# Decode attention and recurrent heads on TensorE: which small products stand next to each other

## The chip, the cores and the metric

The kernel runs on one core of a Trainium2 chip. The metric is the device time of one execution in microseconds (us), from the launch to the end on the core. TensorE (PE) multiplies matrices, VectorE (DVE) and ScalarE (ACT) work on tiles in SBUF and PSUM, GpSimd (POOL) issues the gathers, SyncE (SP) most other DMAs. Each engine has its own stream of instructions and takes them in the order in which the program holds them; semaphores tie the streams together.

## The reference, cut to what matters

One layer of a hybrid decoder, for 512 prompt tokens and for 8 sequences with 4 new tokens each (32 sample tokens), in fp32: a half feed-forward block, a mixer, another half feed-forward block.

```python
h = h + 0.5 * rmsnorm(swiglu(rmsnorm(h, g0), wg[0], wu[0], wd[0]), g1)
m = mixer(rmsnorm(h, g2), ...)          # 4 recurrent heads and 4 latent-attention heads
h = h + rmsnorm(m, g3)
h = h + 0.5 * rmsnorm(swiglu(rmsnorm(h, g4), wg[1], wu[1], wd[1]), g5)
```

Two parts of the mixer matter here. A recurrent head (key and value dimension 128) works in chunks of 64 tokens; within a chunk

```python
b = cumsum(logf)                                   # logf, q, k: (tokens, 128)
A[t, s] = sum_k exp(b[t] - b[s]) * q[t] * k[s]     # s <= t
o = A @ v + (q * exp(b)) @ S                       # S: the state before the chunk
S = exp(b_last) * S + (k * exp(b_last - b)).T @ v
```

The sample tokens of the latent attention see 4096 earlier tokens, held in pages and found through a page table:

```python
keys_c = cache_kv_latent[page_table]     # (8, 4096, 256)
keys_r = cache_k_rope[page_table]        # (8, 4096, 64)
s = (q_lat @ keys_c.T + q_rope @ keys_r.T) / sqrt(192)
o_lat = softmax(s) @ keys_c              # 16 rows (4 tokens, 4 heads) for each sequence
```

## The kernel before, in words

Large products keep fp32 precision by splitting each operand into a high and a low part and adding three products (`mm3`, `gemm_q`, L248). So each weight tile is loaded by SP (`wraw`), rounded by ACT (`wh`) and subtracted by DVE (`wl`, L222); these products, called GEMMs or column products here, are nearly all of TensorE's work. The order of the work is the order in which Python generators are advanced: small work (heads, decode) is placed between pieces of a large one by hand. Some PSUM banks rotate: the list `CYC` gives four banks in turn for all small products (`ps`).

**The recurrent heads** (`hgrn`, L876 on). A head has three generators. `pre` makes q, k, b, v and the gate from column products (512 prompt tokens and 32 sample tokens in two parts of 272), with the transposes of v (L912). `levels` makes A. Since exp(b[t]-b[s]) cannot be split into factors without overflow over a whole chunk, the chunk is split again and again: for each of the decay levels m = 32, 16, 8, 4, 2, 1, `scaled(m)` (L939 to L951) makes a tile `g_E` whose first half of each pair of blocks of m tokens holds k scaled and whose second half holds q scaled; eight products of 64x32 tiles (L971) then give the part of A in which t lies in a second block and s in the first one. Level 0 is the diagonal (L973). Predicated copies put the parts into A (L983, L985), and with products of 32x32 (L977) and copies (L987) the same is done for the sample tokens. The levels are taken in three runs, `RUNL`, each followed by a `yield`; the tiles of the next run are made ahead of the products of the present one, and `g_E` has EB = 4 buffers. `tail` turns k (L1010), makes the states (`pS`, L1026), A times v (L1035), the rest of o, and for the sample tokens the eight state updates (L1069). The function `four` (L888) puts a transpose of the 32 sample tokens on each of the four groups of 32 partitions: once for v in `pre`, once for k in `tail`. The loop over heads advances `levels` and `tail` of one head by one step and then the next head's `pre` by PAT[step] pieces, so that TensorE has column products between the small runs.

**The decode** (L1450 on). The 8 x 4096 past keys are 32 blocks of 1024; a `Half` n (16 of them) is two blocks, half of one sequence. Its life is spread over several rounds of the loop `decode` (L1567 on), each round having five steps st = 0 to 4. In round n:

- `gather` (L1469, POOL, an indirect DMA of 1 MB) fetches a block of latent rows into one of seven slots, `gather_r` (L1476) the rotary keys. After the first ones a block is fetched behind the values that free its slot.
- `turn` (L1484) turns ten groups of 32 key dimensions, two a step in the order `JS`, into `kh`: two DVE transposes of 128x512 (one for each block) a step. The rotary groups come first (`rraw`). `kh` has KHB = 4 buffers, so a turn waits for the scores of four steps earlier.
- `score` (L1496) multiplies the turned keys with the queries, 64x32 tiles, 16 products a step, for half n-2. The table `RUNS` says in which step of the round which of the five scores are issued: three (48 products) at step 2, two (32 products) at step 4. Behind the last, the sums are copied out (L1502, one on ACT, one on DVE) and DVE takes the maximum of each partition (L1504).
- `peak` at step PEAK = 1, for half n-3: TensorE turns the maximum to all partitions (`pm`, L1508, 128x128), DVE reduces it (L1510) and scales it (L1513), ACT takes the exponent (L1514), DVE turns the result (`pt`, L1516), and sixteen copies fill `pbuf` (L1520, four on DVE and twelve on ACT). 
- `value` at step 4, for half n-3: `o`, 2 x 8 products with the latent rows (L1529), and behind the products of each block the next `gather`. For every second half two small products (L1537) and a copy (L1538) follow beside the next `peak`.

A steady round is thus on TensorE: o, some GEMMs, pm, some GEMMs, 48 score products, some GEMMs, 32 score products, the next o. The GEMMs come from `phase_a` (out-projection, first columns of the second feed-forward block, 512 wide), which the main loop (L1627 on) advances beside the decode by a quota for each step (PRE, BODY). `turn` is called at the end of each step; at step 4 it is tied to stand behind the maximum on DVE (`issue_after`). The pipeline starts one turn a step from round 1, step 1, with a gap at round 2: the condition `if n != 2 or st >= 2` leaves out its steps 0 and 1.

## Time and profile before

| | |
|---|---|
| median of three runs | 1236.41 us (1235.94 to 1236.56) |
| the profiled execution | 1235.82 us |
| its span, first to last instruction | 1234.0 us, so 1.8 us lie around it |
| mean granted TensorE clock | 0.995 |
| PE busy over the span | 1207.3 us, 98% |
| DVE busy over the span | 980.4 us, 79% |
| ACT busy over the span | 702.6 us, 57% |
| moved by all DMA in the span | 190.70 MB |

How to read it: the page's parts are the span, each engine's busy time, the span in forty slices, the DMA queues, the shares of the chain that ended last, and the costliest groups of instructions. The timeline lists instructions with their start in us from the span's start, their duration, engine, line, operation, output tile and inputs, tile size, shape and count. A product of two fp32 operands leaves two records for one instruction, so counts of small products are doubled there. Matmuls are pipelined and the end of each is modelled, so the distance from start to start says more than the duration.

### The profile page before, as it was taken

How to read it: one execution, taken by the hardware profiler on the slowest of the kernel's cores; microseconds unless marked ns; L12 is line 12 of the kernel's file. 1: busy time of each engine (PE TensorE's matmuls, PEld its weight loads, DVE VectorE, ACT ScalarE, POOL GpSimd, SP SyncE). 2: the span in 40 equal slices, each digit the busy share in tenths (PEclk: the TensorE clock that was granted, in tenths of full speed). 3: DMA queues.
4: the chain of work that ended last, by engine and by line, in shares of the span. 5: the costliest groups of instructions: out<-in, count | busy, mean ns of one | idle time of the engine just before them, and what ended most of it. 6: DMA issues, size and time to landing. Idle time of an engine off the chain costs nothing.

```text
span 1234.0 us, 29432 instructions
## 1 busy us (share of the span) xinstructions
PE 1207.3 (98%) x12216; PEld 1112.1 (90%) x12216; DVE 980.4 (79%) x1994; ACT 702.6 (57%) x1524; POOL 94.8 (8%) x106
## 2 busy tenths in 40 slices
PE   8999999999999999999999899999999999999997
PEld 7999999999999989988898887777777899999996
DVE  7897787878678787885878789998885779778765
ACT  7675545454376654454758766465555456555373
POOL 0000000000000000000000112332320111000000
PEclk9999999999999999999999999999999999999999
DMA  6232332323254313323342586689774776933551
GB/s 240 86 110 96 103 103 91 99 85 104 65 203 134 116 55 104 89 85 110 99 139 77 158 336 206 220 284 354 276 269 155 263 267 226 223 110 108 113 147 74
DMA packets 80519, 190.70 MB, mean 155 GB/s; under 512 B 14065, under 2 KB 37649, under 8 KB 75905
## 3 DMA queue, kind: packets, MB, share of 16 engines
q1 hardware_dynamic: 58128, 115.50, 28.4%
q0 software_dynamic: 16368, 65.67, 16.3%
q10 hardware_dynamic: 5888, 7.65, 1.9%
q8 instruction: 96, 1.57, 0.5%
q14 instruction: 39, 0.31, 0.1%
HBM read 172.63 MB, written 16.16 MB: 153 GB/s over the span
## 4 chain that ended last, share of the span: by engine, by line
PE 81%; DVE 7%; issue 5%; ACT 4%; DMA 3%; POOL 0%; DVEq 0%; SPq 0%; POOLq 0%
PE acc L248 18%; PE dn L230 12%; PE acc L230 10%; PE Y L449 10%; PE X L449 7%; PE Z L449 6%; PE acc L1833 3%; PE acc L627 3%; PE s L1496 3%; PE o L1529 2%; DVE kh L1484 1%; DMA ma<-w_g 1%; PE pa L971 1%; PE s L1224 1%; DMA wraw<-w_u 1%
## 5 line engine op out<-in xcount | busy, mean ns | idle before, releaser
L248 PE MATMUL acc<-uh,wh 128*128 128x272 f32 (+2 forms) x496 | 161.7, 326 | 0.5 <-ACT uh L195 0.5
L248 PE MATMUL acc<-ul,wh 128*128 128x272 f32 (+2 forms) x496 | 156.6, 316 | 0.9 <-DVE ul L196 0.9
L248 PE MATMUL acc<-uh,wl 128*128 128x272 f32 (+2 forms) x496 | 155.6, 314 | 0.0
L230 PE MATMUL dn<-hh,dh 128*128 128x272 f32 x384 | 111.6, 291 | 0.1
L221 ACT CAST wh<-wraw 128x1024 fp32r<-128x1024 f32 (+2 forms) x78 | 72.6, 932 | 67.1 <-PE acc L248 59.6
L230 PE MATMUL dn<-hh,dl 128*128 128x272 f32 x384 | 110.6, 288 | 0.0
L230 PE MATMUL dn<-hl,dh 128*128 128x272 f32 x384 | 110.5, 288 | 0.0
L222 DVE TENSOR_TENSOR wl<-wraw,wh 128x1024 fp32r<-128x1024 f32 (+2 forms) x78 | 83.7, 1074 | 33.7 <-ACT wh L221 32.9
L248 PEld LDWEIGHTS acc<-uh,wh 128*128 128x128 f32 x496 | 93.3, 188 | 15.2 <-issue 10.1
L248 PEld LDWEIGHTS acc<-ul,wh 128*128 128x128 f32 x496 | 93.4, 188 | 7.1 <-issue 1.6
L248 PEld LDWEIGHTS acc<-uh,wl 128*128 128x128 f32 x496 | 93.3, 188 | 6.1 <-issue 1.1
L230 PEld LDWEIGHTS dn<-hh,dh 128*128 128x128 f32 x384 | 72.3, 188 | 1.3 <-DVE hb L498 0.3
L230 PEld LDWEIGHTS dn<-hl,dh 128*128 128x128 f32 x384 | 72.5, 189 | 0.0
L230 PEld LDWEIGHTS dn<-hh,dl 128*128 128x128 f32 x384 | 72.1, 188 | 0.0
L158 ACT CAST wh<-wraw 128x512 fp32r<-128x512 f32 (+1 forms) x67 | 41.0, 650 | 40.0 <-PE Z L449 22.4
L158 ACT CAST sh<-wraw 128x512 fp32r<-128x512 f32 (+1 forms) x66 | 40.6, 657 | 37.6 <-PE Z L449 26.0
L158 ACT CAST dh<-wraw 128x512 fp32r<-128x512 f32 x48 | 29.8, 621 | 45.8 <-PE dn L230 44.2
L159 DVE TENSOR_TENSOR wl<-wraw,wh 128x512 fp32r<-128x512 f32 (+1 forms) x67 | 46.9, 723 | 7.6 <-ACT wh L158 7.1
L1520 ACT COPY pbuf<-pt 32x64 f32<-32x64 f32 x192 | 46.5, 242 | 8.4 <-DVE pt L1516 5.6
L1496 PE MATMUL s<-kh,q 64*32 64x128 f32 x2560 | 49.1, 273 | 2.0 <-issue 2.0
L1496 PEld LDWEIGHTS s<-kh,q 64*32 64x32 f32 x2560 | 37.5, 105 | 13.4 <-issue 8.0
L159 DVE TENSOR_TENSOR sl<-wraw,sh 128x512 fp32r<-128x512 f32 (+1 forms) x66 | 46.6, 733 | 1.9 <-ACT sh L158 0.8
(721 smaller groups left out, 4109.2 us busy)
## 6 DMA issues: line engine op xcount, KB each, us to landing
wraw<-w_u SPq DMA_DIRECT2D x44, 512.0 KB, 4.2
wraw<-w_g SPq DMA_DIRECT2D x43, 512.0 KB, 3.5
wraw<-w_d SPq DMA_DIRECT2D x24, 512.0 KB, 4.4
wraw<-w_in SPq DMA_DIRECT2D x24, 512.0 KB, 3.9
wraw<-w_o SPq DMA_DIRECT2D x16, 512.0 KB, 3.6
wraw<-w_d SPq DMA_DIRECT2D x16, 384.0 KB, 3.1
wraw<-w_d SPq DMA_DIRECT2D x16, 256.0 KB, 4.5
mA<-sit ACTq DMA_DIRECT2D x14, 256.0 KB, 3.1
```

The costliest lines, as they stand in the source:

```text
L158: nc.scalar.copy(hi, src)
L159: (eng or nc.vector).tensor_tensor(lo, src, f32(hi), op=ALU.subtract)
L221: nc.scalar.copy(wh[:, :kt], w[:, :kt])
L222: low[0] = nc.vector.tensor_tensor(wl[:, :kt], w[:, :kt], f32(wh[:, :kt]), op=ALU.subtract)
L230: nc.tensor.matmul(out, a, b, start=n == 0, stop=n == last)
L248: nc.tensor.matmul(acc[:, :n], a[:, k], b[:, k], start=k + i == 0, stop=k == kt - 1 and i == 2)
L449: nc.tensor.matmul(bank, a[p][:, k], b[q][:, k], start=first and k + n == 0, stop=k == 3 and n == 2, skip_group_check=True)
L627: nc.tensor.matmul(accs[x, d], wts[d][p][:, k], hs[k // 2][q][:, k % 2, x], start=k + n == 0, stop=k == nf - 1 and n == 2)
L1496: nc.tensor.matmul(self.s[r][c * 32 : c * 32 + 32, :P], q[rs, j], kh, start=st + jj == 0, stop=st == len(JS) - 1 and jj == 1, skip_group_c ...
L1520: (nc.scalar.copy if g else nc.vector.tensor_copy)(self.p[g * 32 : g * 32 + 32, c // 2, c % 2 * 4 : c % 2 * 4 + 4, self.i * 16 : self.i * ...
L1529: nc.tensor.matmul(o[g : g + 32, :R], self.p[:, c, a], self.craw[c][:, a], start=i + c == 0 and a < 4, stop=i + c == 2 and a >= 4, skip_gr ...
L1833: nc.tensor.matmul(accs[x, d], wts[d][p][:, k], hs[k // 2][q][:, k % 2, x], start=k + n == 0, stop=k == nf - 1 and n == 2)
```

## The change

Two independent edits.

1. The decode: `RUNS` puts the first three scores of half n-2 at step 1, where `peak` of half n-3 stands, and the gap in the turns at round 2 is one step shorter. The last two scores stay at step 4.

2. The recurrent heads: all seven levels are multiplied in one run instead of three. `scaled` is called for all six levels first, with EB = 6 buffers, in three portions with the same number of `yield`s. The gather of the sample tokens' v moves from `pre` to the end of that run, the one of k from the transposes of k to the run of A times v; `gather32` does what `four` and the copy behind it did.

```diff
-EB, RUNL = 4, ((32, 16), (8, 4), (2, 1, 0))
+EB, RUNL = 6, ((32, 16), (8, 4), (2, 1, 0))
-RUNS = {2: (0, 1, 2), 4: (3, 4)}
+RUNS = {1: (0, 1, 2), 4: (3, 4)}
...
-            def four(out, t):
+            def gather32(t, tag):
+                out = ps("tp")
                 for g in range(0, P, TS):
                     nc.tensor.matmul(out[g : g + TS, :P], t[:, TP:], ident, start=True, stop=True, skip_group_check=True)
+                s_ = mk([P, P], F32, tag)
+                nc.scalar.copy(s_, out[:, :P])
+                return s_
...
-                tp = ps("tp")
-                four(tp, v)
-                vs = mk([P, P], F32, "g_vs", 2)
-                nc.scalar.copy(vs, tp[:, :P])
...
-                ops = [scaled(m) for m in RUNL[0]]
-                for i, ms in enumerate(RUNL):
-                    cur = ops
-                    if i + 1 < len(RUNL):
-                        ops = [scaled(m) if m else (k, q) for m in RUNL[i + 1]]
-                    pa = ps("pa")
+                ops = []
+                for ms in RUNL[:-1]:
+                    ops.append([(m, *scaled(m)) for m in ms])
+                    yield
+                ops.append([(m, *(scaled(m) if m else (k, q))) for m in RUNL[-1]])
+                pas = [ps("pa") for _ in range(2)]
...
+                for ms in ops:
+                    for m, kx, qx in ms:
...
+                vs = gather32(H["v"], "g_vs")
+                for m, po in outs:
...
-                tp = ps("tp")
-                four(tp, k)
-                ks = mk([P, P], F32, "g_ks")
-                nc.scalar.copy(ks, tp[:, :P])
...
                     nc.tensor.matmul(o[es, c * P : (c + 1) * P], A[es, c], vn[es, c], start=c == 0, stop=c == 0, skip_group_check=True)
+                ks = gather32(k, "g_ks")
...
-                        if n != 2 or st >= 2:
+                        if n != 2 or st >= 1:
                             turn(at(2).top if at(2) and st == len(JS) - 1 else None)
```

The lines of the decode move up by two (L1484 is L1482 after, L1496 is L1494, L1508 is L1506, L1510 is L1508, L1516 is L1514, L1529 is L1527); of the heads, L971 is L972, L973 is L974, and L888 is L889.

What the edits do to the order is shown at three places. First TensorE in the second recurrent head, at its last run of level products (`pa` is the PSUM tile of A, `acc` that of a column product). Before:

```order
L248 MATMUL acc<-uh,wl 128x272
L971 MATMUL pa<-g_E 64x32 x16
L973 MATMUL pa<-g_q,g_k 64x64 x8
L977 MATMUL pa<-g_E 32x32 x2
L977 MATMUL pa<-g_q,g_k 32x32
L248 MATMUL acc<-uh,wh 128x272
```

And now, at the only run of level products of that head:

```order
L248 MATMUL acc<-uh,wl 128x272
L972 MATMUL pa<-g_E 64x32 x48
L974 MATMUL pa<-g_q,g_k 64x64 x8
L977 MATMUL pa<-g_E 32x32 x2
L977 MATMUL pa<-g_q,g_k 32x32
L889 MATMUL tp<-ident,g_f 32x128 x4
L248 MATMUL acc<-uh,wh 128x272
```

The 32 products of two earlier runs and the gather of v have moved into this one. In the first head eight of the 48 stand apart.

Next TensorE in the decode, around the product that turns the maximum of half 10 (`s` holds the scores, `q_8207` the queries, `acc` a GEMM). Before:

```order
L248 MATMUL acc<-uh,wl 128x512
L1508 MATMUL pm<-ident,mxh 128x128
L1537 MATMUL o<-q_8207,q_8242 128x32 x2
L248 MATMUL acc<-uh,wh 128x512
L248 MATMUL acc<-ul,wh 128x512
L248 MATMUL acc<-uh,wl 128x512
L248 MATMUL acc<-uh,wh 128x512
L248 MATMUL acc<-ul,wh 128x512
L248 MATMUL acc<-uh,wl 128x512
L1496 MATMUL s<-kh,q_8207 32x128 x48
```

And now:

```order
L248 MATMUL acc<-uh,wl 128x512
L1494 MATMUL s<-kh,q_8203 32x128 x48
L1506 MATMUL pm<-ident,mxh 128x128
L1535 MATMUL o<-q_8203,q_8238 128x32 x2
L248 MATMUL acc<-uh,wh 128x512
```

The run of 48 scores has moved past six GEMMs and past pm; it stands directly ahead of pm.

Last DVE in the decode, from the maximum of half 10 to the reduction of its pm and what follows (`kh` are turned keys, `dx0`, `dx1`, `q0`, `ha` slots of gathered blocks, `rraw` rotary keys). Before:

```order
L1504 TENSOR_REDUCE mxh_11399<-q1_8207 128x1
L1484 STREAM_TRANSPOSE kh_11422<-dx0_11009 128x512
L1484 STREAM_TRANSPOSE kh_11422<-dx1_11214 128x512
L1484 STREAM_TRANSPOSE kh_11431<-dx0_11009 128x512
L1484 STREAM_TRANSPOSE kh_11431<-dx1_11214 128x512
L1484 STREAM_TRANSPOSE kh_11468<-dx0_11009 128x512
L1484 STREAM_TRANSPOSE kh_11468<-dx1_11214 128x512
L1510 TENSOR_REDUCE q1_8207<-pm_11440 128x16
L1538 COPY q0_8242<-o_11205 128x4x16
L1513 SCALAR_TENSOR_TENSOR mq_11443,mbd_11444<-q1_8207 128x16
L1516 STREAM_TRANSPOSE pt_11447<-q1_8207 128x256
```

And now:

```order
L1502 TENSOR_REDUCE mxh_11398<-q1_8203 128x1
L1482 STREAM_TRANSPOSE kh_11421<-dx0_11008 128x512
L1482 STREAM_TRANSPOSE kh_11421<-dx1_11213 128x512
L1482 STREAM_TRANSPOSE kh_11430<-dx0_11008 128x512
L1482 STREAM_TRANSPOSE kh_11430<-dx1_11213 128x512
L1482 STREAM_TRANSPOSE kh_11521<-dx0_11008 128x512
L1482 STREAM_TRANSPOSE kh_11521<-dx1_11213 128x512
L1482 STREAM_TRANSPOSE kh_11530<-rraw_11333 128x512
L1482 STREAM_TRANSPOSE kh_11530<-rraw_11335 128x512
L1482 STREAM_TRANSPOSE kh_11554<-q0_8238 128x512
L1508 TENSOR_REDUCE q1_8203<-pm_11493 128x16
L1536 COPY q0_8238<-o_11204 128x4x16
```

Nine transposes instead of six stand between the maximum and the reduction; the tenth, of the second block in `ha`, stands between the reduction and `pt`. Before, the last four of these stood behind `pt` and behind the next maximum.

More of the change, by code (lines that the diff above doesn't have):

```diff
@@ L954, in up @@
                     return t.rearrange("p (n t m) -> p n t m", t=2, m=m)[:, :, 1]
[L956 to L964 removed]
+                ops = []
[4 more added lines that the diff above has]
+                pas = [ps("pa") for _ in range(2)]
+                outs = []
+                col = 0
+                for ms in ops:
+                    for m, kx, qx in ms:
                         w = 32 if m else CH
[L966 removed]
+                        po = pas[col // 512][:, col % 512 : col % 512 + 4 * w].rearrange("p (c t) -> p c t", c=4)
                         col += 4 * w
[L968 removed]
+                        outs.append((m, po))
                         for c, e, es, cs in chunks():
@@ L973, in levels @@
                                 nc.tensor.matmul(po[es, c], kx[:, cs], qx[:, cs], start=True, stop=True, skip_group_check=True)
-                    if min(ms) <= 2:
-                        pb = ps("pa")
-                        for j, (kx, qx) in enumerate(cur):
-                            nc.tensor.matmul(pb[:TS, j * TS : (j + 1) * TS], kx[:, TP:], qx[:, TP:], start=True, stop=True, skip_group_check=True)
-                    for j, (m, po) in enumerate(zip(ms, outs)):
-                        l = (LEVELS + (0,)).index(m)
-                        if m:
-                            Av = A.rearrange("p c (n t m) -> p c n t m", t=2, m=m)[:, :, :, 1]
-                            mv = up(msk[:, l], m)[:, None].broadcast_to([P, 4, CH // (2 * m), m])
-                            nc.vector.copy_predicated(Av, mv, po.rearrange("p c (n m) -> p c n m", m=m))
-                        else:
-                            nc.vector.copy_predicated(A, msk[:, l : l + 1, :].broadcast_to([P, 4, CH]), po)
-                        if m <= 2:
-                            nc.vector.copy_predicated(As, msk[:TS, l, :TS], pb[:TS, j * TS : (j + 1) * TS])
-                    yield
-                H.update(A=A, As=As)
+                pb = ps("pa")
+                for j, (m, kx, qx) in enumerate(ops[-1]):
+                    nc.tensor.matmul(pb[:TS, j * TS : (j + 1) * TS], kx[:, TP:], qx[:, TP:], start=True, stop=True, skip_group_check=True)
+                vs = gather32(H["v"], "g_vs")
+                for m, po in outs:
+                    l = (LEVELS + (0,)).index(m)
+                    if m:
+                        Av = A.rearrange("p c (n t m) -> p c n t m", t=2, m=m)[:, :, :, 1]
+                        mv = up(msk[:, l], m)[:, None].broadcast_to([P, 4, CH // (2 * m), m])
+                        nc.vector.copy_predicated(Av, mv, po.rearrange("p c (n m) -> p c n m", m=m))
+                    else:
+                        nc.vector.copy_predicated(A, msk[:, l : l + 1, :].broadcast_to([P, 4, CH]), po)
+                    if m <= 2:
+                        j = RUNL[-1].index(m)
+                        nc.vector.copy_predicated(As, msk[:TS, l, :TS], pb[:TS, j * TS : (j + 1) * TS])
+                yield
+                H.update(A=A, As=As, vs=vs)
             def rows(o, out, n, m):
```

7 lines of the change are left out of this document (1 added, 6 removed).

## The prediction

> **What bounds the kernel now.** I read the page first: the span, the busy shares, the shares of the chain that ended last.
>
> ```profile
> span 1234.0 us, 29432 instructions
> PE 1207.3 (98%) x12216; PEld 1112.1 (90%) x12216; DVE 980.4 (79%) x1994; ACT 702.6 (57%) x1524; POOL 94.8 (8%) x106
> PE 81%; DVE 7%; issue 5%; ACT 4%; DMA 3%; POOL 0%; DVEq 0%; SPq 0%; POOLq 0%
> ```
>
> TensorE is busy 98% of the span and 81% of the last chain. Time goes only if matmuls go, if the joints between kinds of matmul get cheaper, or if TensorE waits less. The view of windows shows the two stages that are edited, first one period of the recurrent heads, then halves 2 to 13 of the decode. Its columns are the window and its length, the busy time of PE, its weight loads, DVE, ACT and POOL, the granted clock, and the DMA's share and GB/s.
>
> ```profile
> 468.95:506.92 37.97, 37.79 (x418) 34.04 (x417) 30.80 (x74) 18.94 (x42) 0.43 (x2) 1.00 0.27 85
> 762.19:918.06 155.87, 152.77 (x2905) 111.87 (x2904) 138.59 (x318) 86.85 (x259) 49.05 (x50) 1.00 0.78 275
> ```
>
> In the first, PE is short of its window by 0.18 us: nothing is late, DVE has 7 us to spare. In the second PE is short by 3.1 us of 156, and DVE works 138.59, 89%. So the recurrent stage is a sum of PE times; the decode is one too, but with a vector engine nearly as full, whose order decides whether PE waits. The clock is full in both.
>
> **Part 1, the recurrent heads.** Here the timeline of TensorE gives the price of a joint: a run of two level products (16 records) and one of four (32 records) between column products, and the plain cadence.
>
> ```profile
> 427.32 0.29 PE L248 MATMUL acc<-uh,wl 128*128 128x272 f32 x1
> ...
> 430.35 0.29 PE L248 MATMUL acc<-uh,wl 128*128 128x272 f32 x1
> 430.57 0.66 PE L971 MATMUL pa<-g_E 128*64 128x32 f32 x16
> ...
> 431.39 0.29 PE L248 MATMUL acc<-ul,wh 128*128 128x272 f32 x1
> ...
> 473.73 0.29 PE L248 MATMUL acc<-uh,wl 128*128 128x272 f32 x1
> 473.95 1.12 PE L971 MATMUL pa<-g_E 128*64 128x32 f32 x32
> ...
> 475.23 0.29 PE L248 MATMUL acc<-ul,wh 128*128 128x272 f32 x1
> ```
>
> From 427.32 to 430.35 stand 24 column products: 0.126 us each. I price a run from the start of the last column product before it to the start of the second one behind it (the first behind still shows the joint), less two cadences. 16 records: 431.39 - 430.35 - 0.252 = 0.79. 32 records: 475.23 - 473.73 - 0.252 = 1.25. So 16 records more cost 0.46, 0.029 each, and 0.79 - 0.46 = 0.33 is the fixed price of a run. By the order the stage had 44 runs between column products and has 36 now (levels joined, gathers of the 32 sample tokens moved in, less a few that the pS products open, since they now fall on both sides of a column product). 8 x 0.33 = 2.6 us.
>
> The eight gathers of the sample tokens (two a head) also stood in another shape than their neighbours:
>
> ```profile
> 423.31 0.29 PE L248 MATMUL acc<-uh,wl 128*128 128x272 f32 x1
> 423.44 0.38 PE L912 MATMUL tp<-ident,g_f 128*128 128x128 f32 x2
> ...
> 423.78 0.29 PE L248 MATMUL acc<-ul,wh 128*128 128x272 f32 x1
> ...
> 424.42 0.29 PE L248 MATMUL acc<-uh,wh 128*128 128x272 f32 x1
> ...
> 424.86 0.43 PE L888 MATMUL tp<-ident,g_f 128*32 128x128 f32 x8
> ...
> 425.44 0.29 PE L248 MATMUL acc<-uh,wl 128*128 128x272 f32 x1
> ```
>
> Two transposes alone: 423.78 - 423.31 - 0.252 = 0.22. Two transposes and the gather: 425.44 - 424.42 - 0.252 = 0.77. The gather costs 0.55 behind 128x128 products. Inside a run of other small tiles its eight records cost 0.23 by the slope above, at most their own 0.43. So it saves between 0.1 and 0.3; I take 0.2, near the slope, since its new neighbours are such records: 8 x 0.2 = 1.6. Together -4.2 us, from -2.5 (fixed part alone) to -5.
>
> What could take this back: six E tiles must now be made before the first level product, and the ten masked copies come in one burst behind the last. The 7 us that DVE has free per head cover both; without that cover the wait could be a microsecond a head, 4 in all. The k gather goes one step later and its copy is read only by the last products of the head. I cost both at nothing.
>
> **Part 2, the decode: fewer joints.** Before, the product that turns the maximum (pm, 128x128) stands alone and the first run of scores (s, 48 products as 96 records) six GEMMs behind it; now they adjoin. By the order the scores stand ahead of pm, not behind. The trace of before has both forms, the second in half 11, where no GEMM fell between.
>
> ```profile
> 833.46 0.39 PE L248 MATMUL acc<-hh,wl 128*128 128x512 f32 x1
> 833.68 0.38 PE L1508 MATMUL pm<-ident,mxh 128*128 128x128 f32 x2
> ...
> 834.14 0.39 PE L248 MATMUL acc<-hl,wh 128*128 128x512 f32 x1
> ...
> 835.06 0.40 PE L248 MATMUL acc<-hh,wl 128*128 128x512 f32 x1
> 835.39 1.59 PE L1496 MATMUL s<-kh,q 64*32 64x128 f32 x96
> ...
> 837.26 0.39 PE L248 MATMUL acc<-hl,wh 128*128 128x512 f32 x1
> ...
> 882.72 0.40 PE L248 MATMUL acc<-uh,wl 128*128 128x512 f32 x1
> 882.95 0.38 PE L1508 MATMUL pm<-ident,mxh 128*128 128x128 f32 x2
> 883.27 1.59 PE L1496 MATMUL s<-kh,q 64*32 64x128 f32 x96
> ...
> 885.13 0.40 PE L248 MATMUL acc<-ul,wh 128*128 128x512 f32 x1
> ```
>
> Cadence here: 835.06 - 834.14 over four products, 0.23. pm alone: 834.14 - 833.46 - 0.46 = 0.22. Scores alone: 837.26 - 835.06 - 0.46 = 1.74. Together 1.96; adjoining, 885.13 - 882.72 - 0.46 = 1.95. Nothing is saved. In every second half pm has two further small products behind it, so I allow up to 0.1 a half: 0 to -1.5, taken as -0.5, near the row.
>
> The page "TensorEngine Tiling (Array Packing)" of the Trainium skill says, under Tiling Modes, Key Properties, that changing the tiling mode drains TensorE. By it each half should save one change of mode; the rows above show the fixed price of a run, as the rule would have it, but no saving where these two adjoin.
>
> **Part 3, the decode: the chain.** pm feeds a chain whose end the next values need: DVE reduces pm, ACT takes the exponent, DVE turns it (pt), 16 copies fill pbuf, then TensorE runs o. Half 10 on TensorE, DVE and ACT, then half 13:
>
> ```profile
> 870.47 0.38 PE L1508 MATMUL pm<-ident,mxh 128*128 128x128 f32 x2
> 878.20 1.07 PE L1529 MATMUL o<-mb,pbuf 128*32 128x256 f32 x16
> 867.97 3.67 DVE L1484 STREAM_TRANSPOSE kh<-dx 128x512 f32<-128x512 f32 x6
> 871.56 0.25 DVE L1510 TENSOR_REDUCE q<-pm 128x16 f32<-128x128 f32 x1
> 872.76 0.45 DVE L1516 STREAM_TRANSPOSE pt<-q 128x256 f32<-128x256 f32 x1 [0.73 <-ACT q L1514]
> 873.70 3.07 ACT L1520 COPY pbuf<-pt 32x64 f32<-32x64 f32 x12
> 911.49 3.07 ACT L1520 COPY pbuf<-pt 32x64 f32<-32x64 f32 x12 [0.51 <-DVE pt L1516]
> 913.29 1.07 PE L1529 MATMUL o<-hb,pbuf 128*32 128x256 f32 x16
> 914.17 0.86 PE L1529 MATMUL o<-mb,pbuf 128*32 128x256 f32 x12
> ```
>
> The last copies fill rows 4 to 7 of the second block, read from the middle of the second run of o: two runs stand 0.88 apart (913.29, 914.17), so the last copy may end 1.32 after o starts. Half 10: 878.20 + 1.32 - 876.77 = 2.75 us to spare. Half 13: 913.29 + 1.32 - 914.56 = 0.05. It is the tightest half, and has twelve GEMMs between pm and o where half 10 has eighteen.
>
> Now the scores stand ahead of pm, so pm starts 1.74 later against o, and the spare falls by 1.74 less what the chain no longer waits for. That is nothing: on DVE, eight or nine transposes, not six, stand between the maximum and the reduce (scores free their kh buffers sooner). One takes 3.67 / 6 = 0.61, so nine end 5.5 after 867.97, at 873.5; pm, 1.74 later at 872.2, would be reduced at 873.3 if the lag stayed at 871.56 - 870.47 = 1.09. The reduce loses about 0.2, and what follows it 0 to 0.5, as one or two transposes stand between it and pt, mostly under the 0.73 that DVE waits there for ACT. Where a weight split stands there too it is a further microsecond. Queued behind: the reduce for the chain, and behind the chain o, the end of TensorE's half.
>
> Half 10 keeps 2.75 - 1.74 - (0.2 to 0.7) = 0.3 to 0.8: covered, barely. Half 13 lacks 1.7 to 2.4. By the order of after, four of the fourteen steady halves have only twelve GEMMs from pm to the second scores. Half 13 was the tightest, so I estimate 1.25 for each: 5 us. The other ten are like half 10 with a spare near zero, some short where a split stands in the way; 0.25 each, 2.5 us.
>
> Two more effects, both unseen in before. The turn of a half's second block stands up to eight transposes earlier on DVE, ahead of pt. Its gather is issued only behind the half's o:
>
> ```profile
> DMA to landing us min/median/max: 5.4/8.2/13.6
> 868.46 0.95 POOL L1469 DMA_INDIRECT ha<-pool_c,idx  x1 [0.30 <-issue]
> 881.04 0.67 DVE L1484 STREAM_TRANSPOSE kh<-ha 128x512 f32<-128x512 f32 x1
> ```
>
> From issue to use were 12.6 us; at some 5 less, 7.6, a landing at the median of 8.2 is 0.6 late, one of 13.6 by 6. But only landings above 7.6 hurt, and there the reduce ahead may be late anyway: I take 0.5 in all, and keep 0 to 12 for the range. Below nothing: were PE's 3.1 us in this window all waits that the sooner transposes remove, the decode would gain them; I keep -1.
>
> Sum of the decode's chain: 5 + 2.5 + 0.5 = +8, from -1 to +16. The profiled execution took 1235.8 us (span 1234.0 and 1.8 around it), 0.6 below the median of the runs, 1236.4. -4.2 - 0.5 + 8 = +3.3: 1239.1 against the execution, 1239.7 against the median. A difference of 0.2%, 2.5 us, is about what a measurement of this kernel can tell from none: 1233.9 and 1238.9 are the bounds.
>
> **The rivals.**
> Covered chain (0.22): DVE's freed time behind pt (no transposes stand between pbuf and the next maximum any more) lets each half start its chain sooner, and only the joints count: -4.7, 1231.7. For it: PE hardly waits in before; against it: half 13's 0.05.
> A change of mode has its full price (0.05): the 0.33 of part 1 saved in 15 halves, 4.9 in place of 0.5: 1239.7 - 4.4 = 1235.3. Against it stands half 11. It is the rule of the Trainium skill's page on tiling taken at its word.
> Balance (0.19): only the four short halves pay, 5 - 4.7 = +0.3: 1236.7.
> Gathers decide (0.17): where the second block lands after some 7.6 us from its issue, DVE stands at that transpose with pt queued behind. About half of fourteen landings are later, by 0.6 to 6; at 1 us each this adds 7: 1246.7. For it: DMA is busy 0.78 in this window.
> That the change doesn't do what it says applies to part 2: adjoining, it saves nothing; this is in the forecast.
>
> **How the numbers follow.** Forecast, 0.37: 1239.7, from 1237 to 1243, so 0.10 of it within 0.2% and 0.27 above. Covered chain: 0.22 faster. Mode price: 0.02 faster, 0.03 same. Balance: 0.02 faster, 0.14 same, 0.03 slower. Gathers: 0.17 slower. Faster 0.26, same 0.27, slower 0.47. The range leaves out the far halves of the two outer cases: 1230.5 to 1249.
>
> **What would show it.** In the profile after: the four heads shorter by about 1 us each, with PE still busy throughout; adjoining scores and pm at 1.9 to 2.0 together; between the maximum and the reduce 5 to 6 us of DVE; TensorE standing before o for pbuf, in the short halves by 1 us or more; the decode longer by 6 to 9. I am wrong if o never waits (then the covered chain), if DVE's wait ahead of pt names a gather in many halves (then 1247), or if the heads are not shorter, because the E tiles come late.

## The result, and the profile after

Six runs of each kernel: the changed kernel takes 1254.65 us (1252.19 to 1258.15), the kernel before 1236.22 us (1234.69 to 1236.68); the ratio is 1.015, 95% interval 1.0137 to 1.0162. Slower by 18.4 us, where 3.3 were forecast and 1249 was the range's end. The profiled execution took 1252.19 us, the least of the six, and its span is 1250.2; it lies 16.4 us over the profiled execution of before. The page:

```profile
span 1250.2 us, 29449 instructions
PE 1212.9 (97%) x12216; PEld 1107.2 (89%) x12216; DVE 980.2 (78%) x1994; ACT 704.4 (56%) x1524; POOL 92.5 (7%) x106
PE 75%; DVE 8%; issue 7%; ACT 6%; DMA 3%; POOL 0%; DVEq 0%; SPq 0%; ACTq 0%; POOLq 0%
```

The same instructions are done (12216 records of TensorE, 1994 of DVE), TensorE's share of the last chain falls from 81% to 75%. The windows say where. First one head's period in the kernel after, from one run of levels to the next (37.97 us before):

```profile
476.07:513.19 37.12, 37.12 (x417) 33.91 (x416) 30.78 (x75) 19.35 (x42) 0.43 (x2) 1.00 0.29 88
```

Then the decode from the start of o of half 1 to that of half 13, in the kernel before and in the kernel after:

```profile
769.48:913.28 143.80, 140.70 (x2685) 103.13 (x2680) 128.08 (x293) 79.38 (x237) 46.57 (x47) 1.00 0.80 281
```

```profile
767.28:929.00 161.72, 148.54 (x2680) 100.49 (x2680) 129.26 (x298) 81.73 (x243) 43.99 (x46) 1.00 0.73 249
```

A head is 0.85 us shorter and TensorE never waits in it. Twelve halves of the decode are 17.9 us longer with the same work: 13.5 us a half, not 12.0. TensorE stands idle for 13.2 us of them, not 3.1, and DVE is busy 80%, not 89%: no engine is full any more, so the half is bound by a chain of waits. The idle time is 10.1 us of the 17.9. The rest stands in TensorE's busy time though its work is the same, mostly where o takes `pbuf` piece by piece and its records lie farther apart (o is busy 28.5 us in this window, 23.2 before). Priced as in the prediction, which takes both in, the 14 steady runs of 32 scores and o sum to 63.2 us (47.2 before); the 14 of 48 scores, pm and what adjoins to 33.2 (30.4 before; two of them wait a microsecond or more). That is nearly all of the 18.9 us by which the way from o of half 1 to o of half 14 is longer, and 18.9 less the 2.5 that the heads gain is the 16.4.

Half 10 on DVE shows the chain. The first row is its maximum, the last its turned exponent pt:

```profile
879.60 0.42 DVE L1502 TENSOR_REDUCE mxh<-q 128x1 f32<-128x256 f32 x1 [1.97 <-ACT q L1500]
879.94 2.48 DVE L1482 STREAM_TRANSPOSE kh<-dx 128x512 f32<-128x512 f32 x4
882.68 1.30 DVE L1482 STREAM_TRANSPOSE kh<-dx 128x512 f32<-128x512 f32 x2 [0.26 <-PE s L1494]
883.91 1.26 DVE L1482 STREAM_TRANSPOSE kh<-rraw 128x512 f32<-128x512 f32 x2
885.09 0.67 DVE L1482 STREAM_TRANSPOSE kh<-q 128x512 f32<-128x512 f32 x1
885.69 0.25 DVE L1508 TENSOR_REDUCE q<-pm 128x16 f32<-128x128 f32 x1
...
887.09 0.71 DVE L1482 STREAM_TRANSPOSE kh<-ha 128x512 f32<-128x512 f32 x1 [0.93 <-DMA ha<-pool_c,idx]
...
888.29 0.43 DVE L1514 STREAM_TRANSPOSE pt<-q 128x256 f32<-128x256 f32 x1
```

And the same half on TensorE, then ScalarE:

```profile
881.90 1.59 PE L1494 MATMUL s<-kh,q 64*32 64x128 f32 x96
883.43 0.49 PE L1506 MATMUL pm<-ident,mxh 128*128 128x128 f32 x2
...
888.48 1.16 PE L1494 MATMUL s<-kh,q 64*32 64x128 f32 x64
890.18 1.09 PE L1527 MATMUL o<-mb,pbuf 128*32 128x256 f32 x16 [0.55 <-DVE pbuf L1518]
```

```profile
889.05 3.07 ACT L1518 COPY pbuf<-pt 32x64 f32<-32x64 f32 x12
892.14 0.27 ACT L1500 COPY q<-s 128x128 f32<-128x128 f32 x1
```

Four transposes follow the maximum at once, the fifth waits 0.26 us for the score run: there are four `kh` buffers, and the scores that free the next ones now stand directly ahead of pm. From 882.68 on five transposes lie in the way, 3.0 us, and the reduction starts at 885.69, 2.26 us behind pm (1.09 before). The maximum is late as well: it waited 1.97 us for ScalarE's copy of the scores, so pm starts 3.40 us behind its end, where 1.74 more than before would be 4.15. One more transpose, which waits for its gather, stands ahead of pt. pbuf is full at 892.12. Without a wait o would start at 889.6, 1.08 behind the scores as in half 10 of before, and its last copy would be wanted 1.32 later: pbuf is 1.2 us late, and the run of scores and o costs 4.47 us in place of 3.15. And the copy of the scores for the next maximum stands behind the twelve copies of pbuf on ScalarE, at 892.14.

Over halves 1 to 13, start of pm to start of the reduction on the timelines is 2.88 us on average (1.36 before), pm to the last copy of pbuf 8.23 (6.70 before). The later reduction can be taken apart. From the end of the maximum to the reduction DVE's queue takes 6.48 us on average (3.90 before): transposes 4.83 (3.45), other work such as weight splits and the feed-forward block's elementwise products 1.33 (0.53), idle 0.39 (none before; the rows overlap by 0.1). pm starts 3.60 us behind the maximum (2.54 before). So the queue grew by 2.6 us and pm moved back by 1.1. DVE's list of waits in the decode (sum in us, times, longest) has the late maximum far above the transposes that wait for a buffer:

```profile
DVE mxh L1502 <- ACT q L1500: 14.2, 9, 2.4
DVE kh L1482 <- PE s L1494: 1.6, 3, 0.7
```

### The profile page after: what moved, and what is told of

Read it like the earlier page. It is cut to its first block, busy times and chain, and to the rows that moved or that the text cites. A ratio compares the mean times of both kernels' runs of the same rounds, so it can differ in the third digit from the quotient of the medians.

```text
span 1250.2 us, 29449 instructions
## 1 busy us (share of the span) xinstructions
PE 1212.9 (97%) x12216; PEld 1107.2 (89%) x12216; DVE 980.2 (78%) x1994; ACT 704.4 (56%) x1524; POOL 92.5 (7%) x106
## 3 DMA queue, kind: packets, MB, share of 16 engines
q0 software_dynamic: 16368, 65.67, 16.4%
## 4 chain that ended last, share of the span: by engine, by line
PE 75%; DVE 8%; issue 7%; ACT 6%; DMA 3%; POOL 0%; DVEq 0%; SPq 0%; ACTq 0%; POOLq 0%
PE acc L248 15%; PE dn L230 11%; PE Y L449 10%; PE acc L230 9%; PE X L449 7%; PE Z L449 7%; DVE kh L1482 3%; PE acc L1831 3%; PE acc L627 3%; ACT pbuf L1518 3%; DMA ma<-w_g 1%; PE pa L972 1%; PE s L1222 1%; PE s L1494 1%; DMA ha<-pool_c,idx 1%
## 5 line engine op out<-in xcount | busy, mean ns | idle before, releaser
L1494 PEld LDWEIGHTS s<-kh,q 64*32 64x32 f32 x2560 | 38.1, 105 | 17.1 <-issue 8.7
L1494 PE MATMUL s<-kh,q 64*32 64x128 f32 x2560 | 51.4, 273 | 1.6 <-issue 0.6
```

The source lines that it names most:

```text
L1494: nc.tensor.matmul(self.s[r][c * 32 : c * 32 + 32, :P], q[rs, j], kh, start=st + jj == 0, stop=st == len(JS) - 1 and jj == 1, skip_group_c ...
```

## The experiments

They ran in five groups, each on another chip, beside runs of the kernel before. The group matters: before took 1249.3, 1248.3, 1249.8 and 1249.4 us in four groups, and 1236.4 in one. There were two theories at first. Theory D: the transposes that stand ahead of the reduction on DVE are the loss. Theory P, the prediction's own: pm stands 1.74 us later behind the scores, so the window from pm to o is too short.

| kernel | before there | time, us | ratio to before (95%) | pm to reduction | pm to pbuf full | o of half 1 to o of half 14 |
|---|---|---|---|---|---|---|
| before (first profile) | 1236.2 | | | 1.36 | 6.70 | 156.3 |
| after (first profile) | 1236.2 | 1254.7 | 1.015 (1.0137 to 1.0162) | 2.88 | 8.23 | 175.3 |
| e1_heads | 1249.3 | 1246.2 | 0.9975 (0.9966 to 0.9984) | 1.09 | 6.59 | 167.2 |
| e2_decode | 1249.3 | 1255.8 | 1.0062 (1.0046 to 1.0077) | 2.83 | 8.13 | 174.5 |
| e3_pt | 1249.3 | 1250.1 | 1.0004 (0.9993 to 1.0016) | 1.53 | 6.39 | 170.8 |
| e4_peakfirst | 1249.3 | 1252.1 | 1.0024 (1.0015 to 1.0034) | 0.80 | 6.24 | 172.5 |
| e5_after | 1248.3 | 1255.4 | 1.0066 (1.0043 to 1.0089) | 2.77 | 8.08 | 175.9 |
| e6_ecopy | 1248.3 | 1255.2 | 1.0053 (1.0026 to 1.0079) | 2.65 | 8.07 | 176.1 |
| e7_runs | 1248.3 | 1263.7 | 1.0127 (1.0096 to 1.0157) | 2.98 | 8.05 | 182.7 |
| e8_nogather | 1248.3 | 1245.7 | 0.9988 (0.9975 to 1.0000) | 0.95 | 6.40 | 164.0 |
| e9_pt1 | 1236.4 | 1242.3 | 1.0055 (1.0038 to 1.0072) | 1.16 | 6.08 | 163.5 |
| e10_before | 1236.4 | 1237.1 | one run | 1.09 | 6.46 | 159.6 |
| e11_split | 1236.4 | 1234.1 | 0.9980 (0.9969 to 0.9990) | 1.23 | 6.59 | 158.2 |
| e12_apart | 1236.4 | 1240.0 | 1.0029 (1.0014 to 1.0043) | 0.78 | 6.18 | 162.5 |

The last three columns are read from the timelines of the profiled executions, the first two of them as means over halves 1 to 13.

**e1_heads**: after with the decode's two lines as before.

```diff
-RUNS = {1: (0, 1, 2), 4: (3, 4)}
+RUNS = {2: (0, 1, 2), 4: (3, 4)}
-                        if n != 2 or st >= 1:
+                        if n != 2 or st >= 2:
```

> Only the edit of the recurrent heads; the decode as before. In the profile of the changed kernel the same GEMM stands 0.27 us earlier than before when the heads begin and 2.73 us earlier when they end, so both theories expect 2.5 us less than before: ratio 0.998, about 1233.8 us, and no o that waits for pbuf. A rival, that the heads' new end also disturbs the decode behind it, expects part of the loss here: 1238 us or more.

Measured 3.1 us under before. The heads' edit is a gain by itself.

**e2_decode**: before with the opposite two lines, the heads as before.

> Only the edit of the decode; the heads as before. Theory D (order on the vector engine: eight or nine key transposes stand ahead of the reduction of pm and so in a loop maximum, transposes, reduction, exponent, pbuf, copy of the scores, next maximum, that is now longer than TensorE's work of a half) and theory P (order on TensorE: pm stands 1.74 us later, behind the 48 scores, so the window from pm to o is too short) both expect the whole loss here: 19 to 21 us over before, about 1256 us. If the two edits only hurt together, it is below 1245 us.

6.5 us over before in that group, and 1255.8 in absolute time as expected. So all of the loss is the decode's. That it is 6.5 and not 19 lies with the kernel before, which is 13 us slower there. It was not profiled there, but the profile of e1_heads, whose decode has the lines of before, shows what is slower. Its run of 32 scores of half 7 (in brackets the wait ahead of a row and its cause; "issue" is a wait for nothing that the profile shows):

```profile
844.67 1.03 PE L1494 MATMUL s<-kh,q 64*32 64x128 f32 x45
846.06 0.44 PE L1494 MATMUL s<-kh,q 64*32 64x128 f32 x5 [0.36 <-issue]
846.83 0.42 PE L1494 MATMUL s<-kh,q 64*32 64x128 f32 x4 [0.33 <-issue]
847.56 0.48 PE L1494 MATMUL s<-kh,q 64*32 64x128 f32 x10 [0.30 <-issue]
```

TensorE halts after 45 of the 64 records and then after five and four more, for some 0.6 us from the start of one record to the start of the next. The runs of 32 scores and o sum to 58.5 us (47.2 in the first profile of before).

**e3_pt**: after, with the turns from step 2 on tied behind pt, so that six transposes stand ahead of the reduction and none between it and pt.

```diff
-                nc.vector.transpose(pt.rearrange("p a k -> p (a k)"), self.e)
+                self.turned = nc.vector.transpose(pt.rearrange("p a k -> p (a k)"), self.e)
...
-                            turn(at(2).top if at(2) and st == len(JS) - 1 else None)
+                            turn(at(2).top if at(2) and st == len(JS) - 1 else at(3).turned if at(3) and st >= 2 else None)
```

> The changed kernel, TensorE's order kept (48 scores directly ahead of pm), but the turns from step 2 of a round on are tied behind the transpose pt on the vector engine: six transposes ahead of the reduction as in the kernel before, none between the reduction and pt. Theory D: three transposes of 0.6 us and one or two more leave the loop, some 2.5 us of its 13.5, which brings it under TensorE's 12.0 of a half: 1234 to 1240 us. Theory P: pm stands where it stood, the window stays short: 1248 us or more. If late gathers were the cause, also 1248 or more.

1250.1. That is theory P's figure, 1248 or more, but with before 13 us higher in this group it decides nothing. pm to the reduction falls to 1.53 and pm to pbuf to 6.39; 5.7 us under e2_decode, of which the heads are about 3.

**e4_peakfirst**: after, with the loop over the scores moved behind the call of `peak` within the step.

> The changed kernel with the two swapped within the step: pm first, the 48 scores directly behind it. By the order the vector engine then has four transposes ahead of the reduction and at most two between it and pt. Theory D and theory P both expect the loss gone: 1231 to 1236 us (the heads' 2.5 us less than before, and no wait of o). If the adjoining of pm and scores itself, the sooner turns or late gathers were the cause, 1245 us or more.

1252.1: above the forecast of both theories, and where a cost of the adjoining, of the sooner turns or of late gathers was expected. The chain is short (0.80 and 6.24), and o does not wait for pbuf, yet the decode is no faster than in e3_pt. Halts stand in it (5.8 us between o of half 1 and o of half 14), and one long wait, which is taken up below. In this group the two theories could not be told apart.

**e5_after**: the changed kernel itself.

> The changed kernel itself, beside before on the chip of these runs. On the chip of the four runs ahead of this one before took 1249.3 us and not 1236.2, with 3 us of halts more inside its score products that wait for nothing the profile shows. If those halts and the chain's waits fill the same time (TensorE behind a chain that is longer than its own work does not care for a halt), the changed kernel takes what it took at first, 1254 us, whatever before takes: +5 where before is 1249, +18 where it is 1236. If they add up: +18 on either chip.

1255.4, +7.2: the same time as at first, beside a before that is 12 us slower. Halts and chain waits do not add up: from o of half 1 to o of half 14 TensorE's waits for pbuf fall from 7.3 us in the first profile to 1.3, the halts rise from 0.6 to 3.9, and the 14 runs of 32 scores and o sum to 62.5 us (63.2). The changed kernel waits for its chain, and the halts fall into that wait.

**e6_ecopy**: after, with both copies of the score sums on DVE. I had taken the row at 892.14 for the core of the matter: a loop in which late pbuf copies make the next maximum late.

```diff
-                (nc.vector.tensor_copy if r else nc.scalar.copy)(self.e[:, r * P : r * P + P], self.s[r][:, :P])
+                nc.vector.tensor_copy(self.e[:, r * P : r * P + P], self.s[r][:, :P])
```

> The changed kernel, but both copies of the score sums on the vector engine: the one that ScalarE made no longer stands behind its twelve copies of pbuf. Orders of TensorE and of the transposes are as in the changed kernel. Loop theory (the maximum itself comes late because ScalarE copies pbuf until after the scores are done; the lateness of one half is handed to the next): the maximum comes 1 to 2 us sooner, the loop shrinks, 4 to 10 us less than the changed kernel. Theory that the transposes ahead of the reduction alone are the cause: within 2 us of the changed kernel.

0.3 us under e5_after, and o to o is 176.1 against 175.9. The loop theory falls. DVE in half 6 of this kernel, then TensorE, show why:

```profile
826.77 0.42 DVE L1502 TENSOR_REDUCE mxh<-q 128x1 f32<-128x256 f32 x1
...
828.91 0.67 DVE L1482 STREAM_TRANSPOSE kh<-dx 128x512 f32<-128x512 f32 x1
...
832.62 0.71 DVE L1482 STREAM_TRANSPOSE kh<-ma 128x512 f32<-128x512 f32 x1 [0.78 <-PE s L1494]
...
833.97 0.70 DVE L1482 STREAM_TRANSPOSE kh<-dx 128x512 f32<-128x512 f32 x1
834.60 1.26 DVE L1482 STREAM_TRANSPOSE kh<-rraw 128x512 f32<-128x512 f32 x2
835.79 0.25 DVE L1508 TENSOR_REDUCE q<-pm 128x16 f32<-128x128 f32 x1
```

```profile
831.85 1.59 PE L1494 MATMUL s<-kh,q 64*32 64x128 f32 x96
833.37 0.49 PE L1506 MATMUL pm<-ident,mxh 128*128 128x128 f32 x2
```

The maximum is there at once and four transposes end by 829.6. Then DVE has time to spare, and at 832.62 it has waited for the scores that free a buffer. The reduction comes 2.42 us behind pm; in halves 3, 7 and 10, with nine transposes ahead of it, the 2.26 of the changed kernel's half 10 comes again. Over halves 1 to 13 pm now starts 4.70 us behind the maximum (3.60 in the changed kernel), and DVE's idle time ahead of the reduction grows from 0.39 to 1.16 us a half: 5.6 us in all for scores that free a buffer, 7.9 for sums of GEMMs that other work in the queue takes. So an earlier maximum gains nothing: the queue is then held by TensorE's work ahead of pm. From here on this is the theory: the fifth and later transposes cannot start before the scores that stand directly ahead of pm, and the reduction waits for them, whether or not the maximum is early.

**e7_runs**: before with the line RUNS alone. Ten transposes ahead of the reduction.

> The kernel before with the first half of the decode's edit alone: the scores at step 1, but the gap in the turns as before. By the order ten transposes then stand ahead of the reduction, and mostly none between it and pt; in the changed kernel eight or nine and one or two. Loop theory: the sum ahead of pt is the same ten, so within 3 us of the changed kernel plus the heads' 2.5. If the shorter gap (turns one step sooner) were the cause: the time of before.

1263.7, 8.3 us over e5_after, where at most 5.5 were expected. The sooner start of the turns is not the cause. pm to pbuf is 8.05, as in e5_after (8.08). Of the 6.8 us more from o of half 1 to o of half 14, the 14 runs of 48 scores and pm hold 5.2 and those of 32 scores and o 1.5: with the turns a step later the 48 scores wait for their own turned keys, which is part of it (2.3 us in nine waits, 0.5 in three in e5_after).

**e8_nogather**: e1_heads with only the first seven gathers of latent rows; the later halves use what lies in the slots.

> The heads' edit with the decode of before, and of the 32 gathers of latent rows only the first seven: the later halves use the rows that lie in the slots, so the softmax is over the wrong keys and the gathers' 25 MB are left out. Orders of TensorE and the vector engine are as with the heads' edit alone. If the halts of TensorE inside the score products come from the gathers' traffic: they go, and the time falls by as much as before was above 1236 us on this chip, about 10. If not (or if no chain waits for a gather): within 2 us of the heads' edit alone.

2.6 us under before, about like the heads alone. In the list of waits of TensorE in the decode, first e8_nogather, then the heads' edit in a later group (e14_heads), the halts stand in both:

```profile
PE s L1500 <- issue: 5.0, 16, 0.4
```

```profile
PE s L1494 <- issue: 6.3, 17, 0.8
```

So the halts do not come from these gathers, and no chain in the decode of before waits long for one.

**e9_pt1**: e3_pt with `st >= 1`: four transposes ahead of the reduction, all of which have a free buffer.

> The changed kernel, TensorE's order kept, all turns but the first two of a round tied behind the transpose pt: four transposes stand ahead of the reduction (six in e3_pt, eight or nine in the changed kernel), and by the order none of the four waits for the 48 scores to free a buffer. Anchor theory (from the fifth on the transposes wait for a kh buffer that the 48 scores free, which now stand directly ahead of pm, so the reduction follows pm by as many transposes as are left, whenever the maximum came): pm to reduction falls from 2.8 us to 0.4 to 1.0, pbuf is full some 6 us behind pm, o waits for it in the four short halves alone: 5 to 9 us under the changed kernel, with what is left of TensorE's halts. Theory that the turns' number before the next maximum matters, wherever they stand: the transposes now pile up behind pt and hold the next maximum, within 2 us of the changed kernel.

In this group before takes 1236.4, as at first. 1242.3: 5.9 us over before, where the changed kernel in the first group was 18.4 over. pm to the reduction is 1.16 where 0.4 to 1.0 were expected: in halves 4 and 11 it is near 3, behind a weight split and other work that still stand ahead of it, and 0.5 to 0.6 in six of the others. Half 10 on DVE, ScalarE and TensorE:

```profile
871.60 2.48 DVE L1482 STREAM_TRANSPOSE kh<-dx 128x512 f32<-128x512 f32 x4
874.40 0.29 DVE L1508 TENSOR_REDUCE q<-pm 128x16 f32<-128x128 f32 x1 [0.31 <-PE pm L1506]
...
875.88 0.45 DVE L1514 STREAM_TRANSPOSE pt<-q 128x256 f32<-128x256 f32 x1 [0.73 <-ACT q L1512]
```

```profile
877.08 3.08 ACT L1518 COPY pbuf<-pt 32x64 f32<-32x64 f32 x12
```

```profile
878.92 1.32 PE L1494 MATMUL s<-kh,q 64*32 64x128 f32 x64
880.17 1.07 PE L1527 MATMUL o<-mb,pbuf 128*32 128x256 f32 x16
```

DVE now waits for pm and not pm's result for DVE. o goes straight on behind the scores. In 11 of the 14 steady runs the price of 32 scores and o is 3.15 to 3.47 us (3.15 is the price of an undisturbed run). So in these the window from pm to o, with the order on TensorE of the changed kernel, is long enough, and theory P falls for them. What is left is in three runs (7.24, 6.25 and 4.02 us), where the scores wait for their own turns, which now stand behind pt. They are halves 4, 11 and 13, three of the four halves with only twelve GEMMs behind pm, so for these three the window by itself is not tested; the fourth, half 6, costs 3.47. The waits of TensorE in this decode:

```profile
PE s L1494 <- DVE kh L1482: 5.3, 7, 1.6
```

**e10_before**: the kernel before, for its profile on this chip.

> The kernel before on a chip of the later runs, for its profile. If the 12 us by which it is slower here come from TensorE's halts in the score products: sums of the 14 runs of 32 scores and o near 58 us (47 at first), all else as at first, o not waiting for pbuf.

Before was not slow in this group: the runs of 32 scores and o sum to 49.0 us, near the 47.2 of the first. The halts go with the group of runs. No chip was used in two of these five groups, so the chip and whatever else differs between groups cannot be told apart.

**e11_split** and **e12_apart**: e1_heads with other rows in the table.

```diff
-RUNS = {2: (0, 1, 2), 4: (3, 4)}
+RUNS = {2: (0, 1, 2), 3: (3,), 4: (4,)}
...
+RUNS = {2: (0, 1, 2), 3: (3, 4)}
```

> The heads' edit with the decode of before, but the last two scores one step apart: 16 products, six GEMMs, 16 products and o, so that the run of small products ahead of o is 64 records and not 96. If the halts of 0.6 us come when a long run of small products uses up what TensorE has been given ahead: most go, 6 to 10 us less than the heads' edit alone where before is near 1249, less 14 joints of 0.33, 4.6 us: 1 to 6 us less in all. If they are tied to a place or a time and not to the run's length: 4 to 5 us more than the heads' edit alone.

> The heads' edit with the decode of before, but all 32 last scores one step sooner, six GEMMs ahead of o. The maximum comes 1.4 us sooner, the run ahead of o is 32 records of o alone. If long runs bring the halts: most go, 14 joints of 0.33 are added, 2 to 6 us less than the heads' edit alone where before is near 1249. If not: 4 to 5 us more. The chain has more spare than before in both.

In this group they have few halts to remove. e11_split is 2.3 us under before, no better than the heads alone elsewhere. Its halves price at 0.79 + 2.66 in place of 3.15, so a joint costs 0.30, and there is hardly a halt, where e10_before lost 1.9 us in each of two. e12_apart is 3.6 us over before; the joint costs it 0.2 (1.28 + 2.06), and some of its score and value runs take 0.4 to 1.9 us longer. Whether shorter runs help where halts are many was not tried.

**e13_after, e14_heads, e15_pt2, e16_first, e17_first, e18_heads**: after, e1_heads, e3_pt and e4_peakfirst once more on one chip, then e4_peakfirst and e1_heads on another, in the hope of a group without halts. Before took 1249.8 and 1249.4 us there.

> The changed kernel beside the three others of this call. Anchor theory (the reduction follows pm by the transposes that wait for the scores' buffers): about 1254 us on any chip, pm to reduction 2.7 to 2.9 us, pbuf full 8.1 us behind pm; 17 to 19 us over before where before is near 1236, 5 to 7 where it is near 1249.

> The heads' edit alone: 2.5 us under before on any chip, since nothing of it hangs on the decode.

> The changed kernel with six transposes ahead of the reduction and none between it and pt, on a chip where the kernel with four stood at 1242. Anchor theory: two of the six end behind pm, pm to reduction 1.5 us, pbuf full 6.4 us behind pm where scores and o want it after some 7: 1238 to 1245 us where before is near 1236, far from the changed kernel's 1254. Theory that the window from pm to o is too short by itself (pm 1.74 us later): 1248 us or more there.

> The changed kernel with pm first and the 48 scores directly behind it, on a chip without the halts. The reduction has no transpose that waits for the scores ahead of it, pm stands as early as in before. Anchor theory and window theory: o waits for pbuf nowhere; left are the joints (nothing) and the heads: 1233 to 1236 us where before is near 1236. If it is 1240 or more, something else in the sooner scores costs, such as scores that wait for their own turns, or the gathers.

> The changed kernel with pm first and the 48 scores directly behind it, once more, for a chip on which before takes 1236 us. There: 1233 to 1237 us if the transposes ahead of the reduction are all that the decode's edit costs; 1240 or more if something else of the sooner scores costs too. On a chip where before takes 1249: 1 to 3 us over it, as in the two runs before.

> The heads' edit alone, for the chip of the run beside it: 2.5 to 3.5 us under before on either kind of chip.

| kernel | time, us | ratio to before (95%) | o of half 1 to o of half 14 |
|---|---|---|---|
| e13_after | 1255.0 | 1.0042 (1.0027 to 1.0058) | 175.3 |
| e14_heads | 1246.4 | 0.9972 (0.9962 to 0.9981) | 169.0 |
| e15_pt2 | 1249.2 | 0.9993 (0.9982 to 1.0005) | 171.1 |
| e16_first | 1250.9 | 1.0009 (1.0000 to 1.0019) | 171.1 |
| e17_first | 1251.1 | 1.0007 (0.9994 to 1.0020) | 170.8 |
| e18_heads | 1243.5 | 0.9964 (0.9949 to 0.9980) | 164.2 |

The changed kernel takes 1255 us for the third time, whatever before takes. The heads alone gain again, twice. With pm first the chain is gone (o waits for pbuf nowhere), yet the kernel stays 4 to 8 us over the heads alone. A good 3 us of that stand in one place that the heads alone do not have: once, ahead of o of half 2, the attention's products of L1446 wait for the copy of L1536 on DVE, and their run costs 4.06 us in e16_first, 0.84 in e14_heads. The wait, from e16_first:

```profile
PE o L1446 <- DVE q L1536: 2.6, 1, 2.6
```

The runs of 32 scores and o, halts included, sum to 59.3 us in e16_first and 59.4 in e14_heads of the same group; 58.0 and 55.7 in the last group. What the kernel would be without halts stays open.

## Why the prediction was wrong

The heads (-4.2 forecast, -2.5 to -5): the same GEMM stands 0.27 us earlier when they begin and 2.73 when they end, so -2.5; the three runs of the heads alone give ratios of 0.9964 to 0.9975, 3 to 4.5 us. The joint was priced rightly. The one run of levels, in the kernel after:

```profile
475.85 0.29 PE L248 MATMUL acc<-uh,wl 128*128 128x272 f32 x1
476.07 2.99 PE L972 MATMUL pa<-g_E 128*64 128x32 f32 x96
...
480.24 0.28 PE L248 MATMUL acc<-ul,wh 128*128 128x272 f32 x1
```

480.24 - 475.85 - 0.25 = 4.14 with the gather of v in it, where the three runs took 1.25 + 1.25 + 2.05 = 4.55: two joints of 0.33 saved, 0.24 for the gather. No E tile came late. The term I had too small is the pS products that are now cut in two: the transposes and pS at a head's end cost 2.64 us in head 2 before with the gather of v, and 2.73 without it. With that gather's 0.55 gone, the cut costs 0.64 there.

The joints of the decode (-0.5, from 0 to -1.5): right in size. Scores and pm adjoining take 1.94, with the two small products 2.39, as the rows of before had it. The Trainium skill ("TensorEngine Tiling (Array Packing)", Tiling Modes, Key Properties) says that a change of tiling mode drains TensorE. The prediction misread what that means here: it expected one change less in each half. In the rows pm is 128*128 as the GEMMs are, and the scores are 64*32, so there are two changes whether pm adjoins or not, and by the rule nothing is saved either; the trace agrees. Where the number of changes does differ, so does the time: in the first head some products of 32 columns fell among those of 64, which makes two changes more, and its run of levels takes 441.85 - 437.10 - 0.25 = 4.50 us where the second head's takes 4.14 for the same products.

The chain (+8, from -1 to +16; measured +18.9 from o of half 1 to o of half 14): here it failed, and the step is the sentence "The reduce loses about 0.2". It lost 1.5 us on average, at least 0.8 in each of halves 1 to 13, and "half 10 keeps 0.3 to 0.8" became a lack in eleven of fourteen. That o would wait for pbuf was right; how much the chain grows was not. Three things were wrong in the step:

- I gave the transposes 1.74 us more ahead of pm. But pm moved back by only 1.1 against the maximum, since the maximum came later too.
- I counted transposes alone. They did grow, by 1.4 us, but the other work that the scheduler put ahead of the reduction grew by 0.8 and DVE's idle time there by 0.4. The prediction had named the weight split and given it a quarter of a microsecond in some halves.
- I counted nine transposes from the maximum on, as if each had its buffer. Four can start. From the fifth on each needs a buffer that the scores free, and the change had moved these scores to stand directly ahead of pm. In the changed kernel this wait is mostly hidden behind the late maximum; e6_ecopy shows it as the floor, 2.26 us behind pm for nine transposes however early the maximum is. "Scores free their kh buffers sooner" was used to explain why more transposes stand there, and not to ask when they can start.

On DVE the instructions are taken in the order of the program, so the reduction could not pass any of them; the Trainium skill says so ("TensorE: Matmul & The Clock Gate", section "Architectural detail: the array is 16× 32×32, not 1× 128×128", calls ScalarE's and VectorE's queues strict FIFO), and the reduction 2.26 us behind pm agrees. e9_pt1 shows that this queue is the cause: the order on TensorE is that of the changed kernel, only transposes are taken out from ahead of the reduction, and o stops waiting for pbuf. A run with more than four `kh` buffers, which would price the wait for buffers by itself, was not made.

In the terms of the sum, over the 3.15 us of an undisturbed run of scores and o: the four short halves cost 9.1 us where 5 were forecast, the other ten 10.0 where 2.5 were (before itself stood 3.1 over it in all). The 2.8 us in the runs of 48 scores and pm were not forecast.

The window by itself (5 us for the four short halves) is not shown either way. In e9_pt1 it cost at most 0.2 us in each of the ten long halves and 0.3 in half 6, and the other three short halves waited for something else. The reduction stood 1.09 us behind pm in half 10 of before because of DVE's transposes; without any in the way it needs 0.5, and that pays for a third of the 1.74. That the late reduction would have cost as much with pm where it was is not shown either; in half 10 it takes both, pm's later start 1.6 us and the reduction 1.2, with 1.2 more up to the full pbuf, to turn 2.75 us of spare into 1.2 of lack. (For half 13 the prediction's own terms give a lack of 1.9 to 2.4, not 1.7 to 2.4.)

The rivals: balance did not come, and the price of a mode rested on the misread rule. The gathers, which I gave 1246.7 and 0.17, have the nearer time and not the mechanism: DVE waited once, 0.93 us, for a gather, and leaving the gathers out takes no more from the decode of before than groups differ by (164.0 us, 164.2 to 169.0 in the three runs of the heads alone). The covered chain is what e9_pt1 comes near in eleven halves, with the order on DVE changed. The range was too narrow because all its cases added 0 to 1.25 us for a half; the fourteen halves stood 1.4 us over an undisturbed run on average.

## What to carry to other kernels

When a step is moved on one engine, ask for each instruction, of whatever kind, that a scheduler then puts ahead of a waiting one not only how long it takes but what it waits for: a transpose that waits for a buffer freed by the moved step carries the move into the queue of another engine. A queue ahead of a critical instruction should hold only work that is ready; tie the rest behind it, and look that it does not starve its own readers. Before a difference of one percent is explained, run the kernel before in the same group of runs.

## What the runs showed of the hardware

One kernel differed by 1% between groups of runs. Before took 1236 us in two of the six groups and 1248 to 1250 in the other four (in one of these from 1242.7 to 1250.4 within the group). Each of the last five groups ran on a chip of its own, so whether the chip makes the difference is not shown. The granted clock was the same (0.99 to 1.00). Most of the difference stands in the runs of 64 score records and 32 of o, in which TensorE halts some 0.6 us at a time after about 45 records, with nothing that the profile shows to wait for: 58.5 us in e1_heads, 47.2 in the first profile of before. The runs of 96 score records alone kept their 1.73 us in e1_heads. The gathers of latent rows do not bring the halts. What does is open. The changed kernel, which waits for its chain in the same places, took 1255 us in all three groups in which it ran.

In these kernels the number of changes between tile shapes goes with the price of a run of small products: 0.33 us for a run of levels, which makes two (the prediction's fixed price), 0.36 for two more within such a run (4.50 and 4.14 us), 0.3 for the two that e11_split adds, 0.2 for the one that e12_apart adds. That the change of shape itself is what costs is an inference from these four.
